# A binary search for the 256th score on one Trainium2 core: the short steps of three score tiles done at once, and the next candidate prepared apart

## The chip, the cores and the metric

The kernel runs on one core of a Trainium2 chip. The metric is the device time of one execution in microseconds (us), lower is better. Five engines each work through an instruction list of their own, in order: PE (matrix multiply), DVE (vector), ACT (scalar functions), POOL and SP; DMA queues move data, started by SP and ACT. An instruction that needs a result of another one waits for a semaphore, also where both stand on the same engine.

## The reference, cut to what matters

The reference is a two-layer encoder trunk over 1024 positions of width 1024. Its first layer has a sparse attention: sixteen small index heads give each query a score for every key, and only the 256 best keys of a query take part in its attention.

```python
score = jnp.einsum('bqhs,bqh->bqs', jax.nn.relu(s), iw_b.astype(F32) * w_scale)
allowed = key_chunk[None, :] <= (t // CHUNK)[:, None]
score = jnp.where(allowed[None], score, -jnp.inf)
_, sel = lax.top_k(score, top_k)
...
logits = jnp.where(valid[:, None], logits, -jnp.inf)
p = jax.nn.softmax(logits, axis=-1).astype(v.dtype)
return jnp.einsum('bhqk,bqkhd->bqhd', p, v_sel)
```

Beside it in the same layer stands a gated branch (gMLP: u, v, a spatial matrix); both go into one output projection and a feed-forward part. The second layer is a gated recurrence with a feed-forward part.

## The kernel before

Positions are cut into eight tiles of 128 queries (the 128 partitions). Query tile i can see 128 x (i + 1) keys, so tiles 0 and 1 need no search; tiles 2 to 7 have their scores in the float tiles `acc[i]` (named `tri` in the profile), 128 x 384 up to 128 x 1024.

**The search.** For each query (one partition) the 256th largest score is built bit by bit, from the top bit down: 32 rounds. In a round each of the six tiles, in the order `chain = (7, 2, 6, 3, 5, 4)`, gets three steps on DVE. `count` (L504) compares the whole tile with the query's candidate and adds up how many scores reach it, into a column `cnt`; the comparison itself is written to `junk`, of which there is one buffer. The profile shows a count as two records, the pass over the tile and a short `DVE_READ_ACCUMULATOR`. `m` (L521) turns the count into the bit that has to be taken back, or zero. `cand` (L524) joins this with the candidate and sets the next bit; its two other operands, the old candidate and a column of `bits`, are read as one value per partition ("column operands" below). In the first round (L513, L515) and the last (L527) the steps are a little different. DVE's list interleaves the chain: behind the count of one tile stands `cand` of the tile before, then `m` of this tile, then the next count.

**The selection.** With the threshold known, the masks of tiles 2 to 7 are made one after another on DVE (L535 to L540: count of the larger ones, equal ones, a running sum, the mask). Two DVE steps for the operands of head 0 stand in between: L405 (`sq`, behind an ACT step L404) and L411 (`skb`, behind L410 on ACT, which waits for a load of `kd`). Behind the last mask stands `bigi` (L559), a small constant matrix that PE needs to add the masks.

**What runs beside it.** While DVE searches, PE computes the products for the gated branch, for the queries and keys of the attention (stored to `qd`, `kd`) and for the values. Then it turns `u` with transposes (L551, eight groups of four, into four buffers `bank`/`pbank`); each group is split by ACT (L124, `bhi`) and DVE (L125, `blo`), which sets the buffer free. On PE's list the first scores of the attention stand in between: L572/L573 (query x key), then L576 (mask x `bigi`). On DVE, L579 adds the bias and takes the row minimum; ACT takes the exponentials (L582). On DVE's list: masks, `bigi`, four `blo`, L405 of head 1, four `blo`, then L579 of the first tiles. On ACT's list: four `bhi`, L404 of head 1, four `bhi`, the start of the load of `kd` for head 1 (L409), L582 of three tiles, L410 of head 1. PE's order in the attention is written out by hand; the rest is set by a list scheduler.

Of the kernel before, what the change touches and what calls it, by code (L numbers as in the profile page):

```python
# [10 lines left out]
FT = mybir.dt.float32  # L11
FR = mybir.dt.float32r
BF = mybir.dt.bfloat16
I32 = mybir.dt.int32
AF = mybir.ActivationFunctionType
OP = mybir.AluOpType
# [3 lines left out]
P = 128  # L20
# [6 lines left out]
TOPK = 256  # L27
# [11 lines left out]
def trunk(ctx, tc, a, out):  # L39
    nc = tc.nc  # L40
    act, dve, pool, pe = nc.scalar, nc.vector, nc.gpsimd, nc.tensor

    def pool_(name, bufs, **kw):
        return tc.tile_pool(name=name, bufs=bufs, reuse_waits="tile", **kw)
# [21 lines left out]
    def f(ap):  # L66
        return ap.bitcast(FT)
# [188 lines left out]
    with pool_("xp", 1) as xp:  # L256
# [6 lines left out]
        for hf in range(2):  # L263
# [8 lines left out]
            for k in range(KT):  # L272
                pt = bank()
                for i in range(4):
                    pe.matmul(pt[:, i * P:(i + 1) * P], xin[4 * hf + i][:, k * P:(k + 1) * P], dg[i], start=True, stop=True)
                g = g_mix[0][:, k:k + 1]
                act.activation(h[hf][0][:, k], pt, AF.Copy, scale=g)
                dve.scalar_tensor_tensor(out=h[hf][1][:, k], in0=pt, scalar=g, in1=f(h[hf][0][:, k]), op0=OP.mult,
                                         op1=OP.subtract)
# [32 lines left out]
    with tc.tile_pool(name="idx", bufs=1, reuse_waits="tile") as ip, tc.tile_pool(name="idx2", bufs=2, reuse_waits="tile") as ip2:  # L312
# [24 lines left out]
        for s in range(2):  # L337
            dve.tensor_tensor(out=ik2[:, :, s], in0=tm[:, :, 0:64], in1=ss.unsqueeze(2).to_broadcast([P, 8, 64]),
                              op=OP.mult)
        ka = ip.tile([P, T], FR, name="ka")  # L340
        kb = ip.tile([P, T], FR, name="kb")
        for g in range(2):
# [3 lines left out]
            for s, (h_, l_) in enumerate(((ka, kb), (kb, ka))):  # L346
# [3 lines left out]
                                         op0=OP.mult, op1=OP.subtract)  # L350

        for m in range(8):
# [7 lines left out]
            for hf, n in ((0, 256), (1, 512)):  # L360
                o = pbank()
                fm(o[:, 0:n], wt, h[hf], slice(H - n, H))
                c = slice(0, 256) if hf == 0 else slice(256, 768)
# [4 lines left out]
            for i in range(2, 8):  # L368
                n = P * (i + 1)
                for e in range(2):  # L370
# [10 lines left out]
                    else:  # L381
                        dve.scalar_tensor_tensor(out=acc[i], in0=rl[:, 0:n], scalar=iw[:, i, hd:hd + 1], in1=acc[i],
                                                 op0=OP.mult, op1=OP.add)
# [8 lines left out]
    op0 = mix0.enter_context(pool_("op0", 1))  # L392
# [26 lines left out]
    with pool_("gm2", 2) as gp2, pool_("gm", 1) as gp, pool_("bis", 2) as bp, pool_("up", 1) as up_:  # L419
# [72 lines left out]
        bits = bp.tile([P, 32], I32, name="bits", bufs=1)  # L492
        nc.scalar.dma_start(bits, a["c_bits"])


        chain = (7, 2, 6, 3, 5, 4)
        zero = bp.tile([P, 1], FT, name="zero", bufs=1)
        dve.memset(zero, 0.0)

        def count(i, cand):  # L500
            n = P * (i + 1)
            cnt = bp.tile([P, 1], FT, name=f"cnt{i}")
            junk = bp.tile([P, 1024], BF, name="junk", bufs=1)
            dve.tensor_scalar(out=junk[:, 0:n], in0=acc[i], scalar1=cand, scalar2=None, op0=OP.is_ge, op1=OP.add,  # L504
                              accum_out=cnt)
            return cnt

        cand = {}
        for i in chain:
            cnt = count(i, zero)  # L510

            m = bp.tile([P, 1], I32, name=f"m{i}")
            dve.tensor_scalar(out=m, in0=cnt, scalar1=TOPK - 0.5, scalar2=-1.0, op0=OP.is_lt, op1=OP.mult)  # L513
            cand[i] = bp.tile([P, 1], I32, name=f"cand{i}")
            dve.tensor_scalar(out=cand[i], in0=m, scalar1=bits[:, 30:31], scalar2=None, op0=OP.bitwise_xor)  # L515
        for b in range(30, -1, -1):
            for i in chain:
                cnt = count(i, f(cand[i]))

                m = bp.tile([P, 1], I32, name=f"m{i}")  # L520
                dve.tensor_scalar(out=m, in0=cnt, scalar1=TOPK - 0.5, scalar2=float(1 << b), op0=OP.is_lt, op1=OP.mult)  # L521
                c = bp.tile([P, 1], I32, name=f"cand{i}")
                if b:
                    dve.tensor_scalar(out=c, in0=m, scalar1=cand[i], scalar2=bits[:, b - 1:b], op0=OP.bitwise_xor,  # L524
                                      op1=OP.bitwise_xor)
                else:
                    dve.tensor_scalar(out=c, in0=m, scalar1=cand[i], scalar2=None, op0=OP.bitwise_xor)  # L527
                cand[i] = c
        for i in range(2, 8):
            n, t_ = P * (i + 1), f(cand[i])  # L530
            g = bp.tile([P, 1024], BF, name="junk", bufs=1)
# [539 lines left out]
    with tc.manual_schedule(engines={mybir.EngineType.PE, mybir.EngineType.DVE, mybir.EngineType.Activation}):  # L1071
# [10 lines left out]
        for s, (G, c, e) in enumerate(steps):  # L1082
            g, p = s // 8, s % 8
# [13 lines left out]
            if s + 2 < len(steps):  # L1097
                n = steps[s + 2]
# [167 lines left out]
```

## Time and profile before

| | us |
|---|---|
| median of 3 runs (lowest, highest) | 2926.65 (2925.74, 2927.81) |
| the profiled execution: its time | 2925.3 |
| its span, first to last instruction | 2923.5 |
| mean granted PE clock in it, share of full speed | 0.989 |

A profile is one execution. Times in a timeline are counted from the start of the span; a row has start, length, engine, line, operation, what is written and read with sizes, how many instructions, and in brackets how long the engine stood idle before it and what released it. Records on DVE overlap: the next instruction is often recorded as started a little before the one ahead has ended, so lengths on DVE don't add up to elapsed time; distances from start to start do. PEclk is the granted PE clock: 1.00 is 2.4 GHz, 0.50 is 1.2 GHz.

### The profile page before, as it was taken

Reading aid. Unit: us, or ns where it says so; the run is one execution under the profiler, and the core shown is the slowest. Engines: PE = TensorE matmul, PEld = TensorE weight load, DVE = VectorE, ACT = ScalarE, POOL = GpSimd, SP = SyncE. Lnnn points to the kernel's source line nnn. Section 1 sums busy time; section 2 is a strip of 40 time slices with the busy share of each in tenths; the row PEclk is TensorE's granted clock in tenths of the full one; section 3 lists DMA queues with packets and bytes.
Section 4 is the critical chain, followed back from the end, with each engine's and each line's share of the span. In section 5 each row is a group of like instructions: output and inputs, shape, how many; then the busy total and the mean of one; then the engine's idle time right before and its main releaser. Section 6 shows DMA issues by size and latency. Waiting matters only on the chain.

```text
span 2923.5 us, 38902 instructions
## 1 busy us (share of the span) xinstructions
PE 2822.3 (97%) x15172; PEld 2390.0 (82%) x15188; DVE 1893.0 (65%) x3813; ACT 922.5 (32%) x1704; POOL 971.5 (33%) x648
## 2 busy tenths in 40 slices
PE   7989997999999999999899999999999999999998
PEld 6779885788888888888789999888778888888887
DVE  5779998746644444445777777777766444445446
ACT  4555314622211111111255444544322111111112
POOL 3115721466443443433500000000154343443433
PEclk9999998999999999999999999999999999999999
DMA  5301222333111111111322222222342111111112
GB/s 167 97 29 41 80 87 56 97 103 114 58 44 58 49 45 51 48 47 62 116 59 62 67 69 66 77 66 76 123 150 63 44 44 58 49 45 51 48 47 80
DMA packets 243522, 204.08 MB, mean 70 GB/s; under 512 B 9137, under 2 KB 215778, under 8 KB 243338
## 3 DMA queue, kind: packets, MB, share of 16 engines
q1 hardware_dynamic: 230704, 177.68, 19.6%
q10 hardware_dynamic: 12634, 23.90, 2.7%
q8 instruction: 120, 1.97, 0.3%
q14 instruction: 64, 0.52, 0.1%
HBM read 180.01 MB, written 26.26 MB: 71 GB/s over the span
## 4 chain that ended last, share of the span: by engine, by line
PE 74%; DVE 18%; ACT 4%; issue 2%; POOL 1%; DMA 0%; ACTq 0%; POOLq 0%; SPq 0%; DVEq 0%
PE pbank L119 10%; PE pbank L121 10%; PE pbank L120 10%; DVE junk L504 6%; PE dn L119 6%; PE dn L120 6%; PE dn L121 6%; PE bank L119 5%; PE bank L121 5%; PE bank L120 5%; PE lv L981 2%; DVE cand L524 1%; PE twobank L375 1%; PE bank L596 1%; PE pbank L608 1%
## 5 line engine op out<-in xcount | busy, mean ns | idle before, releaser
L119 PE MATMUL pbank<-bhi,whi 128*128 128x512 f32 (+2 forms) x1352 | 522.0, 387 | 3.3 <-DVE xt L656 3.0
L120 PE MATMUL pbank<-blo,whi 128*128 128x512 f32 (+2 forms) x1352 | 522.2, 386 | 0.0
L121 PE MATMUL pbank<-bhi,wlo 128*128 128x512 f32 (+2 forms) x1352 | 522.2, 386 | 0.0
L77 POOL TENSOR_TENSOR wlo<-raw,whi 128x1024 fp32r<-128x1024 f32 x202 | 488.4, 2423 | 12.7
L76 POOL TENSOR_SCALAR whi<-raw 128x1024 fp32r<-128x1024 f32 x202 | 215.2, 1069 | 811.8 <-PE pbank L120 387.2
L705 DVE TENSOR_TENSOR xt<-xt,dn 128x512 f32<-128x512 f32 x352 | 235.1, 683 | 151.4 <-PE dn L121 151.1
L672 DVE SCALAR_TENSOR_TENSOR cy<-pbank,col_cv,cy 128x511 f32<-128x511 f32 (+1 forms) x176 | 130.8, 743 | 293.6 <-ACT cy L671 293.6
L119 PEld LDWEIGHTS pbank<-bhi,whi 128*128 128x128 f32 (+1 forms) x1352 | 254.4, 188 | 55.2 <-POOL whi L76 3.8
L121 PEld LDWEIGHTS pbank<-bhi,wlo 128*128 128x128 f32 (+1 forms) x1352 | 254.6, 188 | 52.1 <-POOL wlo L584 0.2
L120 PEld LDWEIGHTS pbank<-blo,whi 128*128 128x128 f32 (+1 forms) x1352 | 254.8, 188 | 50.6 <-issue 0.2
L672 DVE SCALAR_TENSOR_TENSOR cy<-bank,col_cv,cy 128x511 f32<-128x511 f32 (+1 forms) x176 | 131.8, 749 | 241.5 <-ACT cy L671 238.6
L119 PE MATMUL dn<-ghi,whi 128*128 128x512 f32 x704 | 278.9, 397 | 0.8 <-ACT ghi L693 0.8
L120 PE MATMUL dn<-glo,whi 128*128 128x512 f32 x704 | 279.0, 396 | 0.0
L121 PE MATMUL dn<-ghi,wlo 128*128 128x512 f32 x704 | 278.5, 396 | 0.0
L119 PE MATMUL bank<-bhi,whi 128*128 128x512 f32 x704 | 274.8, 390 | 0.0
L121 PE MATMUL bank<-bhi,wlo 128*128 128x512 f32 x704 | 274.1, 389 | 0.0
L120 PE MATMUL bank<-blo,whi 128*128 128x512 f32 x704 | 273.9, 389 | 0.0
L694 POOL TENSOR_TENSOR glo<-cy,ghi 128x512 fp32r<-128x512 f32 x88 | 114.3, 1299 | 344.7 <-ACT ghi L693 344.7
L184 POOL TENSOR_TENSOR r<-r,mhalf 128x4 f32<-128x4 f32 x24 | 26.8, 1117 | 587.6 <-DVE r L183 587.6
L671 ACT ACTIVATE cy<-bank,col_cv,col_cv 128x512 f32<-128x512 f32 x88 | 68.1, 774 | 473.8 <-PE bank L121 473.8
L672 DVE SCALAR_TENSOR_TENSOR cy<-halo,col_cv,cy 128x1 f32<-128x1 f32 (+1 forms) x176 | 173.9, 988 | 0.0
L504 DVE TENSOR_SCALAR_CACHE_REDUCE junk<-tri,cand 128x1024 bf16<-128x1024 f32 (+1 forms) x186 | 172.6, 928 | 0.0
(325 smaller groups left out, 5895.3 us busy)
## 6 DMA issues: line engine op xcount, KB each, us to landing
raw<-in_ffn_w_up_dram SPq DMA_DIRECT2D x96, 512.0 KB
raw<-in_c_w_in_dram SPq DMA_DIRECT2D x64, 512.0 KB
raw<-in_ffn_w_down_dram SPq DMA_DIRECT2D x48, 512.0 KB
raw<-in_ab_w_in_dram SPq DMA_DIRECT2D x28, 512.0 KB
raw<-in_ab_w_out_dram SPq DMA_DIRECT2D x16, 512.0 KB
raw<-in_c_w_out_dram SPq DMA_DIRECT2D x16, 512.0 KB
xo<-xd ACTq DMA_DIRECT2D x24, 256.0 KB
ts_d<-td ACTq DMA_DIRECT2D x8, 576.0 KB
```

The source lines that it names most:

```text
L76: pool.tensor_scalar(out=hi, in0=raw, scalar1=1.0, scalar2=1.0, op0=OP.mult, op1=OP.mult)
L77: pool.tensor_tensor(out=lo, in0=raw, in1=f(hi), op=OP.subtract)
L119: pe.matmul(o, lhs[0], rhs[0], start=start, stop=False)
L120: pe.matmul(o, lhs[0], rhs[1], start=False, stop=False)
L121: pe.matmul(o, lhs[1], rhs[0], start=False, stop=stop)
L375: pe.matmul(s[:, c0:c0 + cn], q_, ka[:, c0:c0 + cn], start=True, stop=False)
L504: dve.tensor_scalar(out=junk[:, 0:n], in0=acc[i], scalar1=cand, scalar2=None, op0=OP.is_ge, op1=OP.add, accum_out=cnt)
L671: act.activation(y, o, AF.Identity, scale=cw2[:, c:c + 1], bias=cb[:, c:c + 1])
L672: mac = lambda d, s_, w: dve.scalar_tensor_tensor(out=d, in0=s_, scalar=w[:, c:c + 1], in1=d, op0=OP.mult, op1=OP.add)
L694: pool.tensor_tensor(out=lo, in0=yb, in1=f(hi), op=OP.subtract)
L705: dve.tensor_tensor(out=xt[hf][:, m], in0=xt[hf][:, m], in1=o, op=OP.add)
L981: pe.matmul(lv[:, ls], kl[:, l], ex[:, l], start=True, stop=True)
```

## The change

The six tiles are put into two sets of three, (7, 2, 5) and (6, 3, 4). The counts of a set go into three columns of one `cnt` tile. `m` and `cand` are done once for a set, on 128 x 3, no longer once for a tile on 128 x 1. The old candidate with the next bit set (`flip`, L537) is made by an instruction of its own, as soon as the candidate is known; `cand` is then one exclusive-or of `m` and `flip`, a tensor with a tensor (L521), with no column operand. The steps of one set are laid between the counts of the other. `junk` keeps its single buffer. Line numbers behind the search grow by 15 (L535 becomes L550, L559 becomes L574).

```diff
-        chain = (7, 2, 6, 3, 5, 4)
+        sets = ((7, 2, 5), (6, 3, 4))
...
-        for b in range(30, -1, -1):
-            for i in chain:
-                cnt = count(i, f(cand[i]))
-
-                m = bp.tile([P, 1], I32, name=f"m{i}")
-                dve.tensor_scalar(out=m, in0=cnt, scalar1=TOPK - 0.5, scalar2=float(1 << b), op0=OP.is_lt, op1=OP.mult)
-                c = bp.tile([P, 1], I32, name=f"cand{i}")
-                if b:
-                    dve.tensor_scalar(out=c, in0=m, scalar1=cand[i], scalar2=bits[:, b - 1:b], op0=OP.bitwise_xor,
-                                      op1=OP.bitwise_xor)
...
+        def advance(g, b):
+
+            m = bp.tile([P, 3], I32, name=f"m{g}")
+            c_ = cnt[g]
...
+                dve.tensor_scalar(out=m, in0=c_, scalar1=TOPK - 0.5, scalar2=float(1 << b), op0=OP.is_lt, op1=OP.mult)
+                yield
+                c = bp.tile([P, 3], I32, name=f"cand{g}")
+                dve.tensor_tensor(out=c, in0=m, in1=flip[g], op=OP.bitwise_xor)
+                cand[g] = c
+            yield
+
+        flip = {}
+        for b in range(31, -1, -1):
+            for g in range(2):
+                cnt[g] = bp.tile([P, 3], FT, name=f"cnt{g}")
+                for n, i in enumerate(sets[g]):
+                    count(i, zero if b > 30 else f(cand[g][:, n:n + 1]), cnt[g][:, n:n + 1])
+                    if due:
+                        next(due[0])
+                        if n == 1:
+                            due.pop()
+                if 0 < b < 31:
+                    flip[g] = bp.tile([P, 3], I32, name=f"flip{g}")
+                    dve.tensor_scalar(out=flip[g], in0=cand[g], scalar1=bits[:, b - 1:b], scalar2=None, op0=OP.bitwise_xor)
...
+                due.append(advance(g, b))
```

On DVE, in the middle of the search before, three tiles' worth of steps. The numbers behind a name tell one buffer from another, `tri_438`, `tri_433`, `tri_437` are the scores of tiles 7, 2, 6, and `[waits DVE_49]` marks a wait for an earlier instruction of DVE itself:

```order
L504 TENSOR_SCALAR junk,cnt_5134<-tri_438,cand_5097 128x1024
L524 TENSOR_SCALAR cand_5132<-m_5130,cand_5090,bits 128x1 [waits DVE_49]
L521 TENSOR_SCALAR m_5137<-cnt_5134 128x1 [waits DVE_49]
L504 TENSOR_SCALAR junk,cnt_5141<-tri_433,cand_5104 128x384
L524 TENSOR_SCALAR cand_5139<-m_5137,cand_5097,bits 128x1 [waits DVE_49]
L521 TENSOR_SCALAR m_5144<-cnt_5141 128x1 [waits DVE_49]
L504 TENSOR_SCALAR junk,cnt_5148<-tri_437,cand_5111 128x896
L524 TENSOR_SCALAR cand_5146<-m_5144,cand_5104,bits 128x1 [waits DVE_49]
L521 TENSOR_SCALAR m_5151<-cnt_5148 128x1 [waits DVE_49]
```

Two short instructions stand between two counts, both with a wait, and the count has none. On DVE, in the middle of the search now (`tri_434`, `tri_435`, `tri_436` are tiles 3, 4, 5), one round:

```order
L502 TENSOR_SCALAR junk,cnt_4620<-tri_438,cand_4614 128x1024 [waits DVE_49]
L518 TENSOR_SCALAR m_4623<-cnt_4607 128x3
L502 TENSOR_SCALAR junk,cnt_4620<-tri_433,cand_4614 128x384 [waits DVE_49]
L521 TENSOR_TENSOR cand_4627<-m_4623,flip_4618 128x3 [waits DVE_49]
L502 TENSOR_SCALAR junk,cnt_4620<-tri_436,cand_4614 128x768 [waits DVE_49]
L537 TENSOR_SCALAR flip_4644<-cand_4627,bits 128x3 [waits DVE_49]
L502 TENSOR_SCALAR junk,cnt_4633<-tri_437,cand_4627 128x896 [waits DVE_49]
L518 TENSOR_SCALAR m_4636<-cnt_4620 128x3
L502 TENSOR_SCALAR junk,cnt_4633<-tri_434,cand_4627 128x512 [waits DVE_49]
L521 TENSOR_TENSOR cand_4640<-m_4636,flip_4631 128x3 [waits DVE_49]
L502 TENSOR_SCALAR junk,cnt_4633<-tri_435,cand_4627 128x640 [waits DVE_49]
L537 TENSOR_SCALAR flip_4657<-cand_4640,bits 128x3 [waits DVE_49]
```

One short instruction stands between two counts, and each count waits: it writes `junk`, which the count before it wrote too. On DVE, at the end of the search and the start of the selection before:

```order
L504 TENSOR_SCALAR junk,cnt_5211<-tri_435,cand_5174 128x640
L527 TENSOR_SCALAR cand_5209<-m_5207,cand_5167 128x1
L521 TENSOR_SCALAR m_5214<-cnt_5211 128x1
L535 TENSOR_SCALAR junk,need<-tri_433,cand_5188 128x384
L527 TENSOR_SCALAR cand_5216<-m_5214,cand_5174 128x1
L536 TENSOR_SCALAR need<-need 128x1
L537 TENSOR_SCALAR e<-tri_433,cand_5188 128x384
L405 SCALAR_TENSOR_TENSOR sq_3857<-qk,sq_3857 64x1024
L538 SCALAR_TENSOR_TENSOR qk<-ones,e 128x384
L411 TENSOR_TENSOR skb_3859<-qk,ska_3858 128x1024
```

And the same place now:

```order
L502 TENSOR_SCALAR junk,cnt_4683<-tri_435,cand_4679 128x640
L552 TENSOR_SCALAR e<-tri_433,cand_4690 128x384
L518 TENSOR_SCALAR m_4694<-cnt_4683 128x3
L550 TENSOR_SCALAR junk,need<-tri_433,cand_4690 128x384
L521 TENSOR_TENSOR cand_4696<-m_4694,cand_4679 128x3
L551 TENSOR_SCALAR need<-need 128x1
L405 SCALAR_TENSOR_TENSOR sq_3857<-qk,sq_3857 64x1024
L553 SCALAR_TENSOR_TENSOR qk<-ones,e 128x384
L411 TENSOR_TENSOR skb_3859<-qk,ska_3858 128x1024
```

L405 and L411 keep their places behind the first steps of the selection. From there on DVE's list is the old one, and the lists of PE, ACT, POOL and SP are the old ones from end to end.

## Rows read from the trace of the kernel before

**Rows 1.** The page: busy time by engine, the shares by engine of the chain that ended last, and the group of all counts behind the first round (count, sum in us, mean in ns).

```profile
PE 2822.3 (97%) x15172; PEld 2390.0 (82%) x15188; DVE 1893.0 (65%) x3813; ACT 922.5 (32%) x1704; POOL 971.5 (33%) x648
...
PE 74%; DVE 18%; ACT 4%; issue 2%; POOL 1%; DMA 0%; ACTq 0%; POOLq 0%; SPq 0%; DVEq 0%
...
L504 DVE TENSOR_SCALAR_CACHE_REDUCE junk<-tri,cand 128x1024 bf16<-128x1024 f32 (+1 forms) x186 | 172.6, 928 | 0.0
```

**Rows 2.** The timeline of PE around the end of its products: the last of the first four groups of transposes, the first mask, the last group of transposes, the scores of tile 2.

```profile
457.32 0.60 PE L551 MATMUL pbank<-ident,u 128*128 128x128 f32 x4
...
471.31 0.29 PE L576 MATMUL twobank<-mask,bigi 128*128 128x128 bf16 x1 [13.15 <-DVE bigi L559]
...
474.86 1.06 PE L551 MATMUL pbank<-ident,u 128*128 128x128 f32 x4
477.89 0.66 PE L572 MATMUL twobank<-ska,sq 128*128 128x384 f32 x1 [1.97 <-DVE mn L579]
```

**Rows 3.** The table by stretches: busy time of each engine with the number of instructions, granted PE clock, DMA share, GB/s. Three short stretches around the first scores of the attention.

```profile
460.00:462.00 2.00, 0.00 (x0) 0.00 (x0) 1.96 (x2) 0.00 (x0) 0.00 (x0) 0.64 0.00 0
...
476.00:478.00 2.00, 0.11 (x1) 0.14 (x1) 2.00 (x6) 0.78 (x2) 0.00 (x0) 0.50 0.85 242
...
480.00:482.00 2.00, 2.00 (x11) 1.62 (x12) 0.78 (x3) 0.80 (x3) 0.97 (x2) 0.74 0.23 49
```

**Rows 4.** The timeline of DVE in the search: one step of tile 7 and the count of tile 2 behind it, and the count of tile 7 one round later.

```profile
238.93 1.27 DVE L504 TENSOR_SCALAR_CACHE_REDUCE junk<-tri,cand 128x1024 bf16<-128x1024 f32 x1
240.12 0.08 DVE L504 DVE_READ_ACCUMULATOR junk<-tri,cand 128x1 f32 x1
240.12 0.27 DVE L524 TENSOR_SCALAR cand<-m,cand,bits 128x1 int32<-128x1 int32 x1
240.31 0.14 DVE L521 TENSOR_SCALAR m<-cnt 128x1 int32<-128x1 f32 x1
240.37 0.60 DVE L504 TENSOR_SCALAR_CACHE_REDUCE junk<-tri,cand 128x384 bf16<-128x384 f32 x1
...
245.59 1.27 DVE L504 TENSOR_SCALAR_CACHE_REDUCE junk<-tri,cand 128x1024 bf16<-128x1024 f32 x1
```

**Rows 5.** The timeline of DVE at three other places with short instructions: the first count of all, where `m` stands right behind it; the last round, where `cand` has one column operand; and a product of two 128 x 1 tiles in the second layer, with the instruction behind it.

```profile
225.25 1.28 DVE L504 TENSOR_SCALAR_CACHE_REDUCE junk<-tri,zero 128x1024 bf16<-128x1024 f32 x1
226.46 0.08 DVE L504 DVE_READ_ACCUMULATOR junk<-tri,zero 128x1 f32 x1
226.57 0.15 DVE L513 TENSOR_SCALAR m<-cnt 128x1 int32<-128x1 f32 x1
...
436.07 0.20 DVE L527 TENSOR_SCALAR cand<-m,cand 128x1 int32<-128x1 int32 x1
436.20 0.14 DVE L521 TENSOR_SCALAR m<-cnt 128x1 int32<-128x1 f32 x1
...
1501.34 0.16 DVE L925 TENSOR_TENSOR dl<-dl 128x1 f32<-128x1 f32 x1
1501.42 0.25 DVE L926 TENSOR_SCALAR ex<-ex,dl 128x64 f32<-128x64 f32 x1
```

**Rows 6.** The timeline of DVE behind the search: the first step of the selection, the two steps for the operands of head 0, `bigi`, the first `blo`, the step for head 1, the last `blo` and the first L579.

```profile
438.36 0.60 DVE L535 TENSOR_SCALAR_CACHE_REDUCE junk<-tri,cand 128x384 bf16<-128x384 f32 x1
...
439.51 1.22 DVE L405 SCALAR_TENSOR_TENSOR sq<-qk,sq 64x1024 fp32r<-64x1024 f32 x1
...
441.65 1.20 DVE L411 TENSOR_TENSOR skb<-qk,ska 128x1024 fp32r<-128x1024 f32 x1
...
471.03 0.22 DVE L559 TENSOR_SCALAR bigi<-ident 128x128 bf16<-128x128 f32 x1
471.28 0.69 DVE L125 TENSOR_TENSOR blo<-bank,bhi 128x512 fp32r<-128x512 f32 x1
...
473.80 1.22 DVE L405 SCALAR_TENSOR_TENSOR sq<-raw,sq 64x1024 fp32r<-64x1024 f32 x1
...
476.85 0.68 DVE L125 TENSOR_TENSOR blo<-pbank,bhi 128x512 fp32r<-128x512 f32 x1
477.45 0.28 DVE L579 CUSTOM_DVE_ANT_0 whi<-twobank,bias 128x128 f32<-128x128 f32 x1
```

**Rows 7.** The timeline of ACT: the two steps for head 0; the first and the fourth `bhi`, the step for head 1; the eighth `bhi`, the start of the load of `kd` for head 1 (ACTq is ACT as an issuer of DMAs) and the step that reads it.

```profile
414.75 1.06 ACT L404 ACTIVATE sq<-qk 128x1024 fp32r<-128x1024 f32 x1 [3.87 <-DMA qk<-qd]
420.74 1.06 ACT L410 ACTIVATE ska<-qk 128x1024 fp32r<-128x1024 f32 x1 [4.93 <-DMA qk<-kd]
...
457.13 0.59 ACT L124 ACTIVATE bhi<-bank 128x512 fp32r<-128x512 f32 x1
...
458.56 0.63 ACT L124 ACTIVATE bhi<-pbank 128x512 fp32r<-128x512 f32 x1
463.25 1.06 ACT L404 ACTIVATE sq<-raw 128x1024 fp32r<-128x1024 f32 x1 [4.07 <-issue]
...
475.95 0.60 ACT L124 ACTIVATE bhi<-pbank 128x512 fp32r<-128x512 f32 x1 [0.26 <-PE pbank L551]
475.96 1.10 ACTq L409 DMA_DIRECT2D raw<-kd  x2
...
481.76 1.06 ACT L410 ACTIVATE ska<-raw 128x1024 fp32r<-128x1024 f32 x1 [1.20 <-DMA raw<-kd]
```

**Rows 8.** The timeline of SP (as an issuer of DMAs) at the same place: the load of `qd` for head 2.

```profile
475.05 1.09 SPq L403 DMA_DIRECT2D raw<-qd  x2
```

More of the change, by code (lines that the diff above doesn't have):

```diff
@@ L493, in trunk, with count @@
         nc.scalar.dma_start(bits, a["c_bits"])
-        chain = (7, 2, 6, 3, 5, 4)
+        sets = ((7, 2, 5), (6, 3, 4))
         zero = bp.tile([P, 1], FT, name="zero", bufs=1)
         dve.memset(zero, 0.0)
-        def count(i, cand):
+        def count(i, cand, cnt):
             n = P * (i + 1)
-            cnt = bp.tile([P, 1], FT, name=f"cnt{i}")
             junk = bp.tile([P, 1024], BF, name="junk", bufs=1)
@@ L505, in count @@
                               accum_out=cnt)
-            return cnt
-        cand = {}
-        for i in chain:
-            cnt = count(i, zero)
-            m = bp.tile([P, 1], I32, name=f"m{i}")
-            dve.tensor_scalar(out=m, in0=cnt, scalar1=TOPK - 0.5, scalar2=-1.0, op0=OP.is_lt, op1=OP.mult)
-            cand[i] = bp.tile([P, 1], I32, name=f"cand{i}")
-            dve.tensor_scalar(out=cand[i], in0=m, scalar1=bits[:, 30:31], scalar2=None, op0=OP.bitwise_xor)
-        for b in range(30, -1, -1):
-            for i in chain:
-                cnt = count(i, f(cand[i]))
-                m = bp.tile([P, 1], I32, name=f"m{i}")
-                dve.tensor_scalar(out=m, in0=cnt, scalar1=TOPK - 0.5, scalar2=float(1 << b), op0=OP.is_lt, op1=OP.mult)
-                c = bp.tile([P, 1], I32, name=f"cand{i}")
-                if b:
-                    dve.tensor_scalar(out=c, in0=m, scalar1=cand[i], scalar2=bits[:, b - 1:b], op0=OP.bitwise_xor,
-                                      op1=OP.bitwise_xor)
-                else:
-                    dve.tensor_scalar(out=c, in0=m, scalar1=cand[i], scalar2=None, op0=OP.bitwise_xor)
-                cand[i] = c
+        cand, cnt, due = {}, {}, []
@@ new lines, in advance @@
+        def advance(g, b):
+            m = bp.tile([P, 3], I32, name=f"m{g}")
+            c_ = cnt[g]
+            if b > 30:
+                dve.tensor_scalar(out=m, in0=c_, scalar1=TOPK - 0.5, scalar2=-1.0, op0=OP.is_lt, op1=OP.mult)
+                yield
+                cand[g] = bp.tile([P, 3], I32, name=f"cand{g}")
+                dve.tensor_scalar(out=cand[g], in0=m, scalar1=bits[:, 30:31], scalar2=None, op0=OP.bitwise_xor)
+            else:
+                dve.tensor_scalar(out=m, in0=c_, scalar1=TOPK - 0.5, scalar2=float(1 << b), op0=OP.is_lt, op1=OP.mult)
[3 more added lines that the diff above has]
+                cand[g] = c
+            yield
@@ new lines, in trunk @@
+        flip = {}
[11 more added lines that the diff above has]
+                    dve.tensor_scalar(out=flip[g], in0=cand[g], scalar1=bits[:, b - 1:b], scalar2=None, op0=OP.bitwise_xor)
+                elif b == 0:
+                    flip[g] = cand[g]
+                due.append(advance(g, b))
@@ L529, in trunk @@
+        for _ in range(2):
+            next(due[0])
+        cand = {i: cand[g][:, n:n + 1] for g in range(2) for n, i in enumerate(sets[g])}
         for i in range(2, 8):
```

## The prediction

> **What bounds the kernel now.** I read the page first: PE is busy 97% of the span and carries 74% of the chain that ended last, DVE 18%; the counts of the search are the largest piece of that on DVE, 186 of them in 172.6 us [rows 1]. So DVE bounds the kernel in a stretch, not as a whole, and the question is how long that stretch outlasts PE's other work. PE's timeline tells it: PE ends the first four groups of transposes at 457.9, does the first scores, and then stands still from 458.16 for 13.15 us, until DVE has done `bigi` [rows 2]. On DVE the search begins at 225.25 [rows 5] and its steps follow each other without a gap [rows 4]. So a shorter search is worth its saving one for one up to about 13 us; behind that PE's own work, which the change leaves alone, is the bound. This cap, not the saving, sets the forecast.
>
> **The search: what a step costs.** A round takes 245.59 - 238.93 = 6.66 us [rows 4]. Six counts of 0.928 us on average [rows 1] are 5.57 of it; the other 1.09 us are 0.18 for each of six steps. How it comes about is read in one step: the count's accumulator read and `cand` start together at 240.12, `m` follows 0.19 later, the next count 0.06 after that [rows 4]. So between the accumulator read and the next count lie 0.25 us; 0.07 to 0.08 of that lie in the overlap of the records.
>
> In the changed order one short instruction stands there, and the next count waits for the count ahead, since both write `junk`. Three prices are needed.
> - The short instruction: `m` 0.06 [rows 4]; `flip`, with one column operand, as `cand` of the last round, 0.13 (436.07 to 436.20); `cand`, a tensor with a tensor, as the product on line 925, 0.08 (1501.34 to 1501.42) [rows 5]. Three columns for one add two elements to an instruction whose length is nearly all start and end, so I take nothing for them.
> - The wait: no count of before waits for a count. The nearest row is the first `m`, which waits for the count right ahead of it and starts 0.11 behind the accumulator read's start [rows 5].
> - The two together: they run side by side, since the wait is for the count and not for the short instruction, so I take the longer: 0.11, 0.11 and 0.13, for 0.25 now. Were they to add up, the dearest slot would be 0.13 + 0.11 = 0.24, still no loss; were the wait free, the cheapest would be 0.06. A slot above 0.25 is excluded by no row, see the third rival.
>
> A round has two slots of each kind: 2 x (0.14 + 0.14 + 0.12) = 0.80 us saved. Over 31 rounds that is 24.8 us; the first round has fewer short steps both ways and I add nothing. Bounds: 186 slots from 0.06 to 0.24 save 35 to 2 us. I take 25.
>
> The Trainium skill has another price for this: "Vector Engine (DVE) Microarchitecture Reference", section "5.2 Measured stream behaviour on trn2", gives about 75 ns for each built-in instruction beside its columns, after queue overlap. By that, six instructions fewer in 31 rounds save an estimated 14.0 us, and the forecast would just hold. The step above shows 0.25 us for two instructions behind a count, and that decides here.
>
> **Behind the search: the first cap.** DVE would reach the selection at 438.36 - 25 = 413.4 [rows 6]. There its list holds two steps that wait for ACT. L405 needs ACT's `sq`, done at 414.75 + 1.06 = 415.81; L411 needs `ska`, done at 420.74 + 1.06 = 421.80, which itself waited for the load of `kd` [rows 7]. PE's products set when that load can start, so it stays. L411 thus starts at 421.8, where it started at 441.65 [rows 6]: 19.8 us earlier, and about 5 us of the 25 turn into DVE waits that cost nothing more. `bigi` comes at 471.03 - 19.8 = 451.2. PE's first transposes are not done before 456: from there on DVE waits for PE and ACT.
>
> **The second cap: what is late next.** I follow the three chains that leave this place, each with its old durations.
> - DVE: the first `blo` needs the first `bhi`, done at 457.13 + 0.59 = 457.72 [rows 7]; it starts at 457.75, where it started at 471.28: 13.5 earlier. Four `blo` follow at 0.60 each up to 460.2 (each `bhi` is done by then, the fourth at 459.19); L405 of head 1 starts at 460.2 for 473.80, 13.6 earlier. Four more `blo`, and the first L579 at 463.85 for 477.45 [rows 6]: 13.6 earlier. PE's scores of tile 2, which wait for it, come at 464.3 for 477.89 [rows 2].
> - ACT: the step for head 1 stood at 463.25, released inside the selection, which moves it to 443.5 at the earliest; it now follows the fourth `bhi` at once, 459.1 to 460.15, where it ended at 464.3. The last four `bhi` follow every 0.48 us; the eighth starts at 461.5, where PE at half clock let it start at 475.95. The load of `kd` for head 1 is started with it: 461.5 for 475.96 [rows 7], 14.4 earlier.
> - The load: ACT waited 1.20 us for it and went on at 481.76 [rows 7]; this is the wait that ends last there. It shares the DMA engines with the load of `qd` for head 2, started by SP at 475.05 when L405 of head 1 was done [rows 8]; the engines were 85% busy with the two [rows 3]. The one starts 13.6, the other 14.4 us earlier, so the `kd` data lands 13.6 to 14.4 earlier.
>
> From there every engine's list is the old one and each thing waits for another that has moved along; nothing in the lists is tied to absolute time. I take **14.0 us**, the middle of the two loads.
>
> The clock: with PE idle from 458.16 the granted clock was down to 0.64 on average over 460 to 462, then 0.50, and 0.74 over 480 to 482 [rows 3], so the first scores ran at 1.2 GHz. Now PE is idle only from about 460.9 to 464.3. Whether the clock falls in that gap I can't tell; if it doesn't, the scores are up to 1.5 us faster, most of it ahead of the `kd` load and so hidden.
>
> **The rivals.**
> 1. *DVE stays the bound.* PE then still waits for `bigi`, only less. It takes a search that saves under 13.5 us, that is under 0.07 per slot: slots of 0.18 and more, as if the wait were paid behind the short instruction (0.06 + 0.11 = 0.17, 0.08 + 0.11 = 0.19, 0.13 + 0.11 = 0.24; mean 0.20, so 186 x 0.05 = 9.3 us saved). Time 2926.65 - 9.3 = 2917.4. Against it: in rows 4 `m` waits for the same count behind `cand`, and `cand`'s time covers its wait.
> 2. *More than the cap.* The clock stays up, and the half-clock stretch of before goes too: a transposing group of four is 1.06 us long there and 0.60 before the idle time [rows 2], 1.8 us for four groups and an estimated 1.2 for the scores, 3 in all. Time up to 2926.65 - 17 = 2909.6. Against it: most of that stretch lies ahead of the `kd` load's landing, which doesn't care.
> 3. *Slower.* Counts that wait for each other can't start their fetch of the column operand under the short instruction ahead; 0.06 to 0.13 of fetch is then laid bare in each slot (the difference between short steps with and without such operands [rows 4, 5]). It decides from 0.25 per slot on; with 0.24 + 0.06 = 0.30 in all slots it costs 186 x 0.05 = 9.3 us: 2936. Against it: the first count stands behind a wait in both kernels, and its record is 1.28 long, that of a count without one 1.27 [rows 4, 5].
> 4. *It doesn't do what it says.* DVE's list shows one short instruction between counts in every steady round, so I give this nothing; the same for a delay behind the search, where the lists are the old ones.
>
> **How the numbers follow.** The profiled execution took 2925.3 us, 1.8 beside its span of 2923.5, and 1.35 less than the median of 2926.65; less 14.0, its like would take 2911.3, and the median 2912.6. Chances: the forecast (12 to 15.5 us saved, 2911.1 to 2914.6) 0.77; rival 1 0.09, a third of it within 0.2%; rival 2 0.12; rival 3 0.02. The range leaves out the far part of each rival: 2909.0 to 2916.5. A measurement of this kernel can tell about 0.2%, 5.9 us, from no change: faster by more 0.95, within 0.03, slower 0.02.
>
> **What the profile of the changed kernel would show.** A round of about 5.86 us instead of 6.66, and the next count 0.11 to 0.13 behind each accumulator read. DVE idle before L405 and L411, released by ACT, L411 at 421.8. No wait of PE for `bigi`; `bigi` near 451 and the first `blo` near 457.8, DVE idle ahead of it. A PE gap of about 3.4 us before the scores of tile 2, L579 near 463.9, the `kd` load issued at 461.5 and its reader on ACT at 467.3 to 468.2. The forecast is wrong if PE still waits for `bigi` (rival 1: a round over 6.2 us), or if the later stages, equal in their lists, don't move by the same 14 us.

## The result, and the profile after

The change made the kernel slower: 2952.25 us (median of 4 runs, 2951.10 to 2953.44) against 2926.19 (2923.35 to 2927.81), a ratio of 1.0085 with a 95% interval of 1.0073 to 1.0097, some 26 us. The forecast was 14 us the other way. The page of the changed kernel, for its run of 2953.44 us: the span, the busy times, and the group of all counts behind the first round.

```profile
span 2951.6 us, 38706 instructions
...
PE 2826.5 (96%) x15172; PEld 2396.7 (81%) x15188; DVE 1916.3 (65%) x3617; ACT 922.4 (31%) x1704; POOL 971.0 (33%) x648
...
L502 DVE TENSOR_SCALAR_CACHE_REDUCE junk<-tri,cand 128x1024 bf16<-128x1024 f32 (+1 forms) x186 | 174.8, 940 | 0.1
```

DVE has 196 instructions fewer than before and yet 23.3 us more busy time [rows 1]. The counts have only 2.2 of it (174.8 instead of 172.6). The groups of DVE in the stretch from 225 to 480 us show the rest (sum in us, mean in ns):

```profile
L521 DVE TENSOR_TENSOR cand<-m,flip 128x3 int32<-128x3 int32 x60 | 32.2, 536 | 0.0
...
L518 DVE TENSOR_SCALAR m<-cnt 128x3 int32<-128x3 f32 x62 | 25.1, 404 | 0.0
...
L537 DVE TENSOR_SCALAR flip<-cand,bits 128x3 int32<-128x3 int32 x60 | 23.5, 392 | 0.0
```

These means are no lengths that such a step usually has. The view of one tile gives the shortest, the median and the longest (ns):

```profile
L518 DVE TENSOR_SCALAR m<-cnt x62: 152/165/2402, 238.6 to 465.7; 128x3 int32<-128x3 f32 x62
L521 DVE TENSOR_TENSOR cand<-m,flip x60: 150/158/2050, 239.4 to 461.4; 128x3 int32<-128x3 int32 x60
L537 DVE TENSOR_SCALAR flip<-cand,bits x60: 216/226/1798, 234.3 to 456.5; 128x3 int32<-128x3 int32 x60
```

Half of them are as short as hoped, and some are over ten times as long. The timeline of all engines (cut to DVE and POOL) tells which, first three undisturbed steps, then two of the long ones, then what answers to [rows 6]:

```profile
238.57 0.08 DVE L502 DVE_READ_ACCUMULATOR junk<-tri,cand 128x1 f32 x1
238.57 0.17 DVE L518 TENSOR_SCALAR m<-cnt 128x3 int32<-128x3 f32 x1
238.69 0.75 DVE L502 TENSOR_SCALAR_CACHE_REDUCE junk<-tri,cand 128x512 bf16<-128x512 f32 x1
...
239.36 0.16 DVE L521 TENSOR_TENSOR cand<-m,flip 128x3 int32<-128x3 int32 x1
239.48 0.88 DVE L502 TENSOR_SCALAR_CACHE_REDUCE junk<-tri,cand 128x640 bf16<-128x640 f32 x1
...
240.28 0.23 DVE L537 TENSOR_SCALAR flip<-cand,bits 128x3 int32<-128x3 int32 x1
240.42 1.27 DVE L502 TENSOR_SCALAR_CACHE_REDUCE junk<-tri,cand 128x1024 bf16<-128x1024 f32 x1
...
249.51 2.40 POOL L77 TENSOR_TENSOR wlo<-raw,whi 128x1024 fp32r<-128x1024 f32 x1
249.89 0.08 DVE L502 DVE_READ_ACCUMULATOR junk<-tri,cand 128x1 f32 x1
249.89 2.05 DVE L521 TENSOR_TENSOR cand<-m,flip 128x3 int32<-128x3 int32 x1
...
276.10 2.40 POOL L77 TENSOR_TENSOR wlo<-raw,whi 128x1024 fp32r<-128x1024 f32 x1
...
276.12 2.40 DVE L518 TENSOR_SCALAR m<-cnt 128x3 int32<-128x3 f32 x1
...
465.78 0.61 DVE L550 TENSOR_SCALAR_CACHE_REDUCE junk<-tri,cand 128x384 bf16<-128x384 f32 x1
...
498.12 0.22 DVE L574 TENSOR_SCALAR bigi<-ident 128x128 bf16<-128x128 f32 x1
```

At 238 to 240 POOL is idle, and the next count starts 0.12, 0.12 and 0.14 behind the accumulator read: the prediction's three slots. At 249.89 and 276.12 POOL is in its subtraction for `wlo`, and the DVE step ends when that does: 249.89 + 2.05 = 251.94 against 249.51 + 2.40 = 251.91, and 278.52 against 278.50. These are no single cases: in the trace of after 62 of the steps `m`, `cand` and `flip` are longer than 0.32 us, and every one of them ends 0.01 to 0.03 us behind the end of a POOL instruction. In the trace of before 149 of the one-column steps start while a POOL instruction has over 0.4 us to go, and none is longer than 0.28.

The search takes 465.78 - 228.49 = 237.3 us, where it took 213.1 [rows 5, 6]. The sum nearly closes: what the means stand above the medians is 60 x 0.378 = 22.7 for `cand`, 62 x 0.239 = 14.8 for `m` and 60 x 0.166 = 10.0 for `flip`, together 47.5; 213.1, less the predicted 25, plus 47.5, plus 2.2 of longer counts, is 237.8. (The end at 465.78 takes in `e`, a step of the selection that now stands ahead, some 0.3 us.) PE waits for it, in the view of its waits (us in total, times, longest):

```profile
PE twobank L591 <- DVE bigi L574: 27.8, 1, 27.8
PE twobank L587 <- DVE sq L405: 6.9, 1, 6.9
```

It waited 13.15 for `bigi` before [rows 2].

### The profile page after: what moved, and what is told of

Its sections match the earlier page's. It is cut to its first block, busy times and chain, and to the rows that moved or that the text cites. A ratio compares the mean times of both kernels' runs of the same rounds, so it can differ in the third digit from the quotient of the medians.

```text
span 2951.6 us, 38706 instructions
## 1 busy us (share of the span) xinstructions
PE 2826.5 (96%) x15172; PEld 2396.7 (81%) x15188; DVE 1916.3 (65%) x3617; ACT 922.4 (31%) x1704; POOL 971.0 (33%) x648
## 4 chain that ended last, share of the span: by engine, by line
PE 74%; DVE 19%; ACT 4%; issue 2%; POOL 1%; DMA 0%; ACTq 0%; POOLq 0%; SPq 0%; DVEq 0%
PE pbank L119 10%; PE pbank L120 10%; PE pbank L121 10%; DVE junk L502 6%; PE dn L119 6%; PE dn L121 6%; PE dn L120 6%; PE bank L119 5%; PE bank L121 5%; PE bank L120 5%; PE lv L996 2%; PE bank L611 1%; PE twobank L375 1%; PE pbank L623 1%; DVE cand L521 1%
## 5 line engine op out<-in xcount | busy, mean ns | idle before, releaser
L502 DVE TENSOR_SCALAR_CACHE_REDUCE junk<-tri,cand 128x1024 bf16<-128x1024 f32 (+1 forms) x186 | 174.8, 940 | 0.1
```

## The experiments

Theory A: DVE and POOL share a path to their data; a step that needs it waits until the POOL instruction under way has ended. The counts and the one-column steps of before don't need it, the three-column steps do. The runs of the kernel before beside these experiments gave medians of 2927.0 to 2927.9 us.

**POOL silent.** In both kernels, for the stretch of the search:

```
-  POOL makes whi and wlo of the weights        +  ACT makes both (wlo all zeros)
-  POOL multiplies in the gated branch          +  left out, or a copy on ACT
```

> The changed kernel with POOL silent during the search: its splitting of the weights of the gated branch, queries, keys and values goes to ACT (the low parts are left out, written as zeros), and the products of the gated branch on POOL are left out or copied by ACT. Theory A (the 128x3 steps stand still while POOL works, since they want an SBUF path that POOL holds): m, cand and flip fall to 0.15 to 0.23 us each all through the search, the 47 us that they are over those lengths vanish, PE no longer waits for bigi, and the forecast of the prediction holds after all: about 2912 us. Rival B (the waits of the counts or the new order make the steps slow): POOL has no part in it, the steps stay at 0.39 to 0.54 us on average, about 2952 us.

> The kernel before with the same work of POOL left out or moved to ACT as in after_quiet. Theory A: the 128x1 steps of the search never stood still beside POOL, so nothing changes in the search: a round of 6.66 us, about 2926 us, within 4. Rival B says the same; the run shows what leaving out the work is worth by itself, so that after_quiet can be read.

The changed kernel took 2908.73 us (ratio 0.9938, 0.9922 to 0.9953), the kernel before 2920.87 (0.9981, 0.9972 to 0.9991): with POOL silent the change gains 12.1 us. The first is 3 us below what was expected. The second misses its 2926 within 4 by about 1 us, and its profile, of the longest of ten executions (2926.81), doesn't show why; what was expected of the search came out. It takes 437.23 - 224.13 = 213.1 us in the kernel before, as without the edit, and 410.10 - 218.57 = 191.5 in the changed one. So without POOL the change takes 21.6 us out of the search, and POOL puts 237.3 - 191.5 = 45.8 on it. The groups of the short steps in the changed one have no long members left:

```profile
L542 DVE TENSOR_SCALAR flip<-cand,bits 128x3 int32<-128x3 int32 x60 | 13.5, 225 | 0.0
L523 DVE TENSOR_SCALAR m<-cnt 128x3 int32<-128x3 f32 x62 | 10.2, 164 | 0.0
L526 DVE TENSOR_TENSOR cand<-m,flip 128x3 int32<-128x3 int32 x60 | 9.4, 157 | 0.0
```

**One column, but two tensors.** The kernel before, with one step rewritten:

```
-  dve.tensor_scalar(out=c, in0=m, scalar1=cand[i], scalar2=bits[:, b - 1:b], ...)
+  dve.scalar_tensor_tensor(out=c, in0=m, scalar=bits[:, b - 1:b], in1=cand[i], ...)
```

> The kernel before with one thing changed: cand takes the old candidate as a second tensor (128x1) and no longer as a column operand; same number and order of instructions, same waits. Theory A in the form A1 (an instruction with two tensors in SBUF stands still while POOL reads SBUF, whatever its size): 180 steps that stand still as long on average as cand did in the changed kernel (0.54 less 0.16 us), less 0.06 us for the column operand saved: 30 to 57 us slower, 2956 to 2983 us, with lengths up to 2.4 us. Rival C (it is the three columns that are slow, not the second tensor): about 2915 us, since a column operand is saved in each step.

2963.51 us (1.0121, 1.0105 to 1.0138). The group of `cand`, with 180 members:

```profile
L524 DVE SCALAR_TENSOR_TENSOR cand<-m,bits,cand 128x1 int32<-128x1 int32 x180 | 84.7, 471 | 0.0
```

So for `cand` it is not the number of columns: a step with one element per partition stalls, if it has two tensors. The longest took 2449 ns.

**The change, column by column.** Sets, order and waits of the change, but each of `m`, `cand` and `flip` as three one-column steps:

```
-  dve.tensor_tensor(out=c, in0=m, in1=flip[g], op=OP.bitwise_xor)
+  for n in range(3):
+      dve.tensor_scalar(out=c[:, n:n + 1], in0=m[:, n:n + 1], scalar1=flip[g][:, n:n + 1], ...)
```

> The changed kernel with its sets, order and waits, but m, cand and flip each done as three steps on one column, cand with flip as a column operand. Theory A: no step stands still; per round 6 m at 0.06, 6 cand and 6 flip at 0.13 are 1.92 us behind the counts for 1.50 before, 31 x 0.42 = 13 us slower than before: about 2939 us, and no step is longer than 0.3 us. Rival B (order or waits): the 47 us of standing still stay and the 13 come on top of before's time: about 2986 us.

2938.49 us (1.0038, 1.0023 to 1.0053), as theory A had it:

```profile
L542 DVE TENSOR_SCALAR flip<-cand,bits 128x1 int32<-128x1 int32 x180 | 26.8, 198 | 0.0
L524 DVE TENSOR_SCALAR cand<-m,flip 128x1 int32<-128x1 int32 x180 | 26.6, 198 | 0.0
```

`m` has a mean of 137 ns, and no step is longer than 0.23 us. The new order and its waits make no step stall; the 11 us over the kernel before go with 18 short steps in a round for its 12.

**Short POOL instructions.** The changed kernel with

```
-  pool.tensor_tensor(out=lo, in0=raw, in1=f(hi), op=OP.subtract)
+  for s0 in range(0, m, 256):
+      pool.tensor_tensor(out=lo[:, s0:s0 + 256], in0=raw[:, s0:s0 + 256], ...)
```

> The changed kernel, with one edit on POOL: in the stretch of the search the subtraction that makes wlo (one POOL instruction of 128x1024, 2.40 us) is written as four of 128x256; the result is the same. Theory A (a DVE step that uses the path shared with POOL waits until the POOL instruction under way has ended): the longest stall of m, cand and flip falls from 2.4 us to about 1.3 us (the products of 128x512 that are left) and the mean stall of the steps that land on wlo to a quarter; about half of the 47.5 us excess lay there, so 10 to 17 us come back: 2936 to 2943 us, and no m, cand or flip above 1.4 us. Rival D (the stall is DVE's own, a price of three-column steps that only happens to appear in this stretch, or it grows with POOL's busy time rather than with the length of one instruction): POOL is no less busy, so the longest steps stay near 2.4 us and the time near 2952 us.

2931.02 us (1.0013, 1.0004 to 1.0022), 5 us below the range that was expected. The longest `flip` is now 1147 ns, `cand` 1089, `m` 978, as expected; the means stand 33.2 us above the medians instead of 47.5, so 14.3 of the 21 us come from the search. The rest comes ahead of it (in the profiled runs the search starts at 221.67 instead of 228.49, part of which differs from run to run in any case, see the end of the next section), and the same edit in the kernel before shows where:

> The kernel before, with the one edit on POOL of the run with short subtractions (wlo in four pieces of 128x256, from the set-up of the gated branch to the last weight of v). In that run the two-tensor sums of the scores (tri, ahead of the search) were shorter too (mean 1053 ns instead of 1100, 90 of them), and the search began some 3.6 us earlier by them. Theory A: the kernel before already paid for the shared path there, so tri is shorter here as well, the search, which has one-column steps only, keeps its length, and PE's wait for bigi shrinks by about 4 us: 2921 to 2925 us. Rival: POOL is busier by the split (45.4 us instead of 38.4) and the start of the search only varied between runs: 2926 to 2930 us.

2921.95 us (0.9981, 0.9972 to 0.9990). The sums of the scores, which have two tensors as input, are the group that got shorter; first the kernel before, up to 232 us of its span, then this one:

```profile
L382 DVE SCALAR_TENSOR_TENSOR tri<-rl,iw,tri 128x384 f32<-128x384 f32 (+5 forms) x90 | 96.7, 1100 | 11.6 <-ACT rl L378 8.3
```

```profile
L387 DVE SCALAR_TENSOR_TENSOR tri<-rl,iw,tri 128x384 f32<-128x384 f32 (+5 forms) x90 | 92.3, 1054 | 11.3 <-ACT rl L383 8.0
```

That is no chance of single runs: the mean is 1100 or 1101 ns in all eight profiled runs with the long subtraction, 1053 or 1054 in the three with the short ones, and 1020 in the two with POOL silent. The kernel before had thus paid for the same path, 4 us of it ahead of the search.

One step of the expectation missed: PE's wait for `bigi` hardly shrank, 12.6 us for 13.15. PE gained ahead of the search as well, its waits for `rl` and `iq` between 100 and 232 us fell from 9.7 us to 5.3, and it ended its first transposes 6.5 us earlier in this profile. So PE and DVE both came earlier, and the time fell in the range by another way.

**Another layout.** `m` and `flip` of the changed kernel read each column twice, into six elements:

```
-  m = bp.tile([P, 3], ...); c_ = cnt[g]
+  m = bp.tile([P, 6], ...).rearrange("p (n d) -> p n d", d=2)
+  c_ = cnt[g].unsqueeze(2).to_broadcast([P, 3, 2])
```

> The changed kernel, with m and flip written on a shape of [3, 2], each column read twice through a step of zero, so that input and output have six elements in place of three and the two sides differ in layout; cand is the same two-tensor step of three columns. Theory A1 (a one-input step goes the path shared with POOL only in a fast form that this layout rules out; a step with two tensors always goes it): m and flip are 0.15 to 0.25 us with no long ones, cand stays near 536 ns mean; the 24.8 us of excess of m and flip goes, some of it taken over by cand: 2927 to 2936 us. Rival A2 (any step of more than one column stalls): m and flip stay near 400 ns and the time at 2950 to 2954 us.

2930.44 us (1.0009, 1.0000 to 1.0018). `m` and `flip` are short throughout, `cand` with its two tensors stalls as before:

```profile
L522 DVE TENSOR_TENSOR cand<-m,flip 128x3 int32<-128x3 int32 x60 | 35.0, 583 | 0.0
...
L538 DVE TENSOR_SCALAR flip<-cand,bits 128x6 int32<-128x6 int32 x60 | 12.7, 212 | 0.0
L519 DVE TENSOR_SCALAR m<-cnt 128x6 int32<-128x6 f32 x62 | 9.4, 152 | 0.0
```

So the steps with one tensor use the path by their form, and a layout takes them off it; the steps with two tensors used it in every run here that has them beside POOL. That the form of `m` and `flip` is a fast one is theory A1's reading; no record names it.

**A constant in place of a column.** The kernel before, with

```
-  scalar1=cand[i], scalar2=bits[:, b - 1:b]
+  scalar1=cand[i], scalar2=1 << (b - 1)
```

> The kernel before, with one edit: the bit that cand flips comes as a constant in the instruction in place of a column operand (bits); all steps stay on one column. If the second column operand costs what the rows say (cand 261 ns with two, 198 ns with one in the run with the steps column by column), each of 180 steps loses 0.063 us and DVE, which is still the bound, ends its search 11.3 us earlier: 2914 to 2917 us. Rival: the fetch of the second operand is hidden behind the first, or cand waits for the column that m wrote either way: 2924 to 2928 us.

2916.14 us (0.9962, 0.9950 to 0.9975). The timeline of DVE, one step:

```profile
261.53 0.08 DVE L504 DVE_READ_ACCUMULATOR junk<-tri,cand 128x1 f32 x1
261.53 0.21 DVE L524 TENSOR_SCALAR cand<-m,cand 128x1 int32<-128x1 int32 x1
261.65 0.14 DVE L521 TENSOR_SCALAR m<-cnt 128x1 int32<-128x1 f32 x1
261.71 1.00 DVE L504 TENSOR_SCALAR_CACHE_REDUCE junk<-tri,cand 128x768 bf16<-128x768 f32 x1
```

`m` follows `cand` after 0.12 instead of 0.19 [rows 4], and the slot is 0.18 instead of 0.25.

**Both lessons in one kernel.** `m` on the doubled layout, `cand` column by column with the constant, no `flip`:

```
-  dve.tensor_tensor(out=c, in0=m, in1=flip[g], op=OP.bitwise_xor)
+  for n in range(3):
+      dve.tensor_scalar(out=c[:, n:n + 1], in0=m[:, n, 0:1], scalar1=cand[g][:, n:n + 1], scalar2=(1 << b) >> 1, ...)
```

> The sets and the order of the change, with m for three columns on the layout of the run before last (each column twice), and cand column by column as in the kernel before, with the bit as a constant; no flip. No step has two tensors or the fast form, so by theory A1 none waits for POOL: per round two m of about 0.16 us and six cand of about 0.2 us in place of six of 0.13 and six of 0.26, some 26 us less in the search than before, more than PE's end can use: the prediction's own two caps apply, 2911 to 2915 us. If the layout does not keep m off the shared path, 62 m at 0.4 us give 15 us back and PE still waits for bigi: 2918 to 2926 us.

2921.32 us (0.9979, 0.9971 to 0.9988): a miss, and not for the reason that I had given to that case, since `m` is 155 ns throughout. The timeline of DVE, from one `m` to the next accumulator read with no step behind it:

```profile
260.57 0.16 DVE L519 TENSOR_SCALAR m<-cnt 128x6 int32<-128x6 f32 x1
260.69 0.74 DVE L502 TENSOR_SCALAR_CACHE_REDUCE junk<-tri,cand 128x512 bf16<-128x512 f32 x1
...
261.36 0.45 DVE L523 TENSOR_SCALAR cand<-m,cand 128x1 int32<-128x1 int32 x3
261.73 0.87 DVE L502 TENSOR_SCALAR_CACHE_REDUCE junk<-tri,cand 128x640 bf16<-128x640 f32 x1
262.52 0.08 DVE L502 DVE_READ_ACCUMULATOR junk<-tri,cand 128x1 f32 x1
262.64 1.28 DVE L502 TENSOR_SCALAR_CACHE_REDUCE junk<-tri,cand 128x1024 bf16<-128x1024 f32 x1
```

A count that follows an accumulator read with nothing between starts 0.12 behind it, no sooner than one with an `m` between. The three `cand` in one place cost 0.37. I had added up durations again where slots count.

**The same steps, one behind each count.**

```
   for n in range(3):
       dve.tensor_scalar(out=c[:, n:n + 1], ...)
+      if n < 2:
+          yield True      (the next one stands behind the next count)
```

> The steps of the kernel with m on the doubled layout and cand column by column with a constant bit, in another place: one step behind each count (m; cand of column 0; of column 1; cand of column 2 with the other set's m) in place of m, three cand, nothing. Slot theory: behind each count's accumulator read there is about 0.12 us in which one step costs nothing, and every further step costs what it adds; the kernel with three cand in one place paid 0.37 + 0.12 + 0.12 per set (6.42 us per round against 6.30 with one-column steps and the constant). Here a round has four places with one step and two with two, 4 x 0.12 + 2 x 0.19 = 0.86 us in place of 1.22: 6.06 us per round, the search some 7 us shorter than with the constant alone, of which PE can use its last 2.9 us of wait for bigi: 2911 to 2915 us. Rival: a step that stands behind the count it doesn't depend on costs its own length wherever it stands: 2919 to 2923 us, as with three in one place.

2914.08 us (0.9956, 0.9942 to 0.9971). The slots in the timeline of DVE:

```profile
260.03 0.21 DVE L524 TENSOR_SCALAR cand<-m,cand 128x1 int32<-128x1 int32 x1
260.16 1.14 DVE L502 TENSOR_SCALAR_CACHE_REDUCE junk<-tri,cand 128x896 bf16<-128x896 f32 x1
...
261.22 0.21 DVE L524 TENSOR_SCALAR cand<-m,cand 128x1 int32<-128x1 int32 x1
261.35 0.15 DVE L519 TENSOR_SCALAR m<-cnt 128x6 int32<-128x6 f32 x1
261.41 0.74 DVE L502 TENSOR_SCALAR_CACHE_REDUCE junk<-tri,cand 128x512 bf16<-128x512 f32 x1
```

0.13 with one step and 0.19 with two, as the slot theory had it. PE no longer waits for `bigi`; its largest wait here is 3.4 us for the first scores, and DVE now waits for the first `bhi`:

```profile
PE twobank L585 <- DVE mn L592: 3.8, 2, 3.4
```

```profile
458.25 0.69 DVE L125 TENSOR_TENSOR blo<-bank,bhi 128x512 fp32r<-128x512 f32 x1 [4.01 <-ACT bhi L124]
```

**The constant and the short POOL instructions.** The two edits shown above, in the kernel before.

> The kernel before with both one-sided edits: the bit as a constant, and wlo in four pieces on POOL. The constant alone left PE a wait of 2.9 us for bigi; if the search begins some 3 to 4 us earlier by the shorter pieces, that wait is gone and the second cap (PE behind the scores of the blocks) is reached: 2911 to 2914.5 us. If the start does not move, as with the constant alone: 2915 to 2918 us.

2911.31 us (0.9943, 0.9930 to 0.9956), the fastest that leaves no work out, 16 us under the kernel before and 41 under the changed one; its interval overlaps that of the run before it. The wait that was to be gone is not, in its profiled run of 2913.24 us:

```profile
PE twobank L583 <- DVE bigi L566: 2.1, 1, 2.1
```

With the constant alone it was 2.9. As in the run with the short pieces alone, PE came earlier together with DVE; the time is right, the way to it was not.

## Why the prediction was wrong

**The step that failed** is the price of the short instruction: "Three columns for one add two elements to an instruction whose length is nearly all start and end, so I take nothing for them." Where POOL is idle that is right (medians 158, 165 and 226 ns). But the step also changed its kind. `cand` got a second tensor, and `m` and `flip` a form that uses the path shared with POOL; each then lasts until the end of the POOL instruction that it meets. The term that was put at nothing cost some 46 us of search, against 22 saved where 25 were forecast. With POOL silent the loss of 26 us is a gain of 12.1; one-column steps in the same order don't stall; one-column steps with two tensors do; POOL's length sets the longest stall.

**The row that misled.** The price of `cand` came from a product on line 925 at 1501 us [rows 5], where POOL had nothing to do. In the search it has, as the table by stretches of the kernel after shows (length, POOL's busy time with its instructions, granted PE clock, DMA share, GB/s):

```profile
240.00:417.00 177.00, 117.91 (x83) 1.00 0.23 73
```

Two thirds of the stretch in which most of the search lies are POOL's, and in the kernel before it was as much (115.63 us of the same 177). The prediction has no row of POOL, although two-tensor steps beside it were to be found in the trace of before, in its timeline at 703 us:

```profile
703.49 2.40 POOL L77 TENSOR_TENSOR wlo<-raw,whi 128x1024 fp32r<-128x1024 f32 x1
703.85 2.59 DVE L219 TENSOR_TENSOR nacc<-nacc,nsq 128x512 f32<-128x512 f32 x1 [0.76 <-ACT nsq L217]
```

Three and a half times its usual length: the same operation and shape on line 1168 has a mean of 728 ns. The Trainium skill states the rule that was missed: by "SBUF — State Buffer", section "Who interferes with whom", DVE's second port pair is GpSimd's as well; an instruction with two SBUF inputs, or a tensor_scalar in a 2-port mode (not the form with an accumulator output), contends for it, and whichever issues first keeps it for its whole instruction. The trace agrees in each part that was tried: stalls of `cand`, `m` and `flip` up to 2.40 us, none of the counts, and none of the one-column steps with one tensor. Which mode a step ran in no trace here shows.

**"A slot above 0.25 is excluded by no row"**: true, and the third rival had the sign (slower, given 0.02), but another mechanism and a fifth of the price. In the undisturbed slots above no such fetch lies bare. The sum of waits and steps that the first rival rests on isn't there either; the slots were 0.12, 0.12 and 0.14.

**The two caps.** Where the search was short enough, what the prediction followed through the lists came out. The first cap shows only with POOL silent, where DVE stands still ahead of the step `skb` for ACT's `ska`:

```profile
415.47 1.23 DVE L416 TENSOR_TENSOR skb<-qk,ska 128x1024 fp32r<-128x1024 f32 x1 [2.32 <-ACT ska L415]
```

In the run with the steps spread the search still ended too late for it. The second cap was reached there: the first `blo` at 458.25 (predicted near 457.8), the first scores' step on DVE at 464.42 (463.9), the `kd` load issued at 461.48 (461.5) and its reader at 467.64 (467.3 to 468.2), and PE's gap is 3.4 us. The gain was some 13 us, against 14.0. What the prediction couldn't tell of the clock: it was granted in full through the gap (1.00 from 461.4 to 464.8) and then fell to 0.50 between 466 and 468.

**What stays open.** Why the search begins between 224.1 and 228.5 us in profiled runs of equal code ahead of it; 3.2 us of the later end in the profiled run of after are this. And what the remaining stalls of two-tensor steps in the later layers cost was not tried.

## What to carry to other kernels

Before two small DVE steps are merged, ask whether the merged one still has a single tensor input and a one-column form, and what POOL does at that time: the price of a short step taken where POOL is idle says nothing of a stretch where POOL works. A stall here lasted as long as the rest of POOL's instruction, so shorter POOL instructions helped even though they added work. And count slots between long instructions, not durations: one short step behind a count was free here, a second cost 0.06 to 0.13.

## What was not expected of the hardware

- A DVE step of 0.16 us lasts up to 2.40 us beside POOL, and ends within 0.03 us of POOL's instruction. POOL's own subtraction stays at 2.40 us.
- A POOL step with one tensor holds the path as well. In the run with the other layout, in the timeline, `cand` ends at 273.19 and POOL's `whi` at 273.18:

```profile
272.13 1.05 POOL L76 TENSOR_SCALAR whi<-raw 128x1024 fp32r<-128x1024 f32 x1
...
272.37 0.82 DVE L522 TENSOR_TENSOR cand<-m,flip 128x3 int32<-128x3 int32 x1
```

- The sixteen subtractions of the stretch, each cut in four of 128x256, kept POOL busy for 45.4 us, whole for 38.4, and the kernel was still faster.
- Not every POOL instruction holds the path: in the run after, a `cand` that starts at 286.61, inside POOL's 1.66 us on a tile of 128x8 (from 286.06), takes 0.16 us.
- Reading every column twice made `m` no longer: a median of 152 ns for six elements, where three took 165.
